# First feed-forward of a macaron decoder block: two output parts by seven block products, weight sums by adding transfers, a smaller ring, and coefficient steps moved into the mix

## Chip, cores and metric

One core of a Trainium2 chip runs the whole decoder block in one program. The metric is the device time of one execution in microseconds, the median of several runs. All inputs are in HBM at the start, the output is in HBM at the end.

## The reference

The layer works on 512 tokens of 1024 channels, all in float32. A vector c gives nine modulation vectors (shift, scale and gate for three sub-layers); then come a SwiGLU feed-forward, a token mixer (pooling and three groups of dilated attention, gated) and a second feed-forward, each added to the residual h.

```python
D_MODEL, SEQ, D_FF = 1024, 512, 2816
cond = jax.nn.silu(c)
mod = cond @ w_ada[l] + b_ada[l]
sh1, sc1, gt1, sh2, sc2, gt2, sh3, sc3, gt3 = [m[:, None, :] for m in jnp.split(mod, 9, axis=-1)]
u = modulate(rmsnorm(h, g_norm_ffn1[l]), sh1, sc1)
h = h + 0.5 * gt1 * swiglu(u, w_ffn1_in[l], w_ffn1_out[l])
u = modulate(rmsnorm(h, g_norm_mix[l]), sh2, sc2)
h = h + gt2 * token_mixing(u, cos, sin, w_in[l], ...)
u = modulate(rmsnorm(h, g_norm_ffn2[l]), sh3, sc3)
h = h + 0.5 * gt3 * swiglu(u, w_ffn2_in[l], w_ffn2_out[l])
...
def swiglu(u, w_in, w_out):
    a, b = jnp.split(u @ w_in, 2, axis=-1)
    return (jax.nn.silu(a) * b) @ w_out
```

## The kernel before

**Precision.** Everything is kept transposed: channels on the 128 partitions, tokens along the free axis. Each float32 product is made of three products of a shorter type: both operands are split into a high and a low part, and TensorE (PE) adds high times high, high times low and low times high in one PSUM bank. `mm3` issues the three for 512 columns (L390 to L392), `product` for 256 (L787 to L789), `out_blocks` for 256 (L929 to L931). A weight chunk is 128x1024, which is eight 128x128 tiles and so 24 matmuls. ACT writes its high part into the ring `whi` (L346) and DVE its low part into `wlo` (L358). Both rings hold 7 x 1024 + 128 columns. `look(n)` splits chunks up to n beyond the next one; `take` hands out the next chunk.

**Loads.** Chunks come from HBM by transfers on the queue of SP (L266) into three buffers `raw` and, in the feed-forwards, two quarters of `X`. Each engine and each queue works strictly in the order in which the program is written out by hand; nothing reorders at run time.

**Feed-forward.** 22 pairs of tiles (a and b of SwiGLU) are made, and after some of them an output part: `PARTS` are tiles 0-4, 4-8, 8-12, 12-16 and 16-22, each multiplied into all eight output tiles and added to h with the gate. The first four pairs of the first feed-forward run in `startup`, pairs 4 and 5 are plain, the others are made two at a time by `duo`: a product of two 2x2 block matrices by seven block products instead of eight (weight rows in two halves, tokens in two halves). For this the weights need sums of chunks: in the first feed-forward DVE makes four per group of four chunks (L283), in the second it makes two, and two more are made by adding transfers issued by POOL (L291). The output parts 0 to 3 of the second feed-forward are made by seven block products too (`out_blocks`); those of the first are plain (L390 to L392 with `HI` and `HK`, H updated by L1053). Before a duo that follows a plain part stands one settling matmul of 240 columns (L396).

**Coefficients.** The modulation vectors are made beside the rest, in 72 steps of DVE (`ada_do`, L417): each reads 128 rows of w_ada (512 KB, `ada_fetch`, L409, on SP), multiplies by cond and sums. `bg` does the next step and fetches ahead into whatever buffers `ada_free` lists; `ada_stop` is where a stage ends. In the first feed-forward all up to 48 are done: from the second output part on, `bg` is called after H updates, with the buffers `cs` and `AR`. The mix does the rest: three in the loop that makes v1 (with `AR`, `uc` and the parts of `v23`), ten beside attention, three more before the gated merge, and eight beside the mix's output (L1703).

**Start of the mix.** `head` makes the first four query and key tiles. `rope_a` copies each to SBUF with a sign (ACT, L1203), swaps 32-row groups by four transfers on SP (L1206), and multiplies the bank by the cosine (DVE, L1208). Then four token blocks of v1 are made (L1462 to L1465); between them DVE finishes the rotation (`rope_b`, L1214 and L1215). Attention scores (L1252) are put into the middle of the next tile's matmuls. The lines of the loop that matter:

```python
for i in ((), (0, 1), (2,), (3,))[n]:
    self.rope_b(*to[i], 1, sw[i])
if n == 1:
    self.ada_free += [self.v23.rearrange("p n f -> p (n f)")[:, i * D:(i + 1) * D] for i in range(2)]
if n:
    self.bg()
```

The angle tables (`trig`) are made by DVE and ACT (sines, L1181 to L1183) in steps of `todo`, which output parts 2 and 3 of the first feed-forward work off.

Of the kernel before, what the change touches and what calls it, by code (L numbers as in the profile page):

```python
# [131 lines left out]
RING = 7 * 1024 + 128  # L132
# [6 lines left out]
BLOCK_PARTS = {0: (), 2: (0, 1, 2, 3)}  # L139
# [19 lines left out]
class Kernel:  # L159
# [6 lines left out]
    def plan(self):  # L166
# [44 lines left out]
        def ffn(n, ins, outs, first):  # L211
# [248 lines left out]
    def sumsq(self, m, src):  # L460
# [5 lines left out]
        s = self.tp.tile([P, T], F32, name="ut")  # L466
# [24 lines left out]

    def norm_t(self, n, k, hs):
        G = self.mod[:, 24 * n + 8 + k:24 * n + 9 + k]
        t = self.tp.tile([P, T], F32, name="ut")
# [52 lines left out]
    def out_tail(self, ms, ksrc, gate, nxt, squares):  # L547
# [3 lines left out]
        tiles, starts, put = {}, {}, []  # L551
# [3 lines left out]
        for h, hs in enumerate((A, Bh)):  # L555
            for m in ms:
# [12 lines left out]
                for i, (hi, lo, uh, ul) in enumerate(ks):  # L569
                    if h == 1 and m == ms[1] and i == 3:  # L570
                        self.stats_t(self.B[6], A)
                    if h == 1 and m == ms[2] and i == 1:
                        self.spread(self.B[6], A)
# [18 lines left out]
    def out_end(self, ms, ksrc, gate):  # L592
# [5 lines left out]
        rA, rB = (b for b in self.B if not any(b is x for x in self.banks))  # L598
# [12 lines left out]
        for h, hs in enumerate((A, Bh)):  # L611
            for m in ms:
# [20 lines left out]
                s = self.tp.tile([P, T], F32, name="ut")[:, :HT]  # L633
# [34 lines left out]
    def head(self, n, banks, table):  # L668
# [9 lines left out]
        for h, hs in enumerate((A, Bh)):  # L678
            for i, (k, which) in enumerate(steps if h == 0 else [(k, both) for k in range(KT)]):
                if h == 0:  # L680
                    stepA(min(i, 5) + 3)
                    if i == 4:
                        self.stats_t(self.B[7], Bh)
                        nc.scalar.preload_act_table(table)
                    if i == 8:
                        self.spread(self.B[7], Bh)
# [13 lines left out]
    def work(self, name, w):  # L700
        return self.wk[name][:, :w] if self.wk else self.fw.tile([P, w], F32, name=name)

    def ffn_post(self, j, s, pb):
        nc = self.nc
        h = self.wk["hf"][:, j % 2 * T:(j % 2 + 1) * T] if self.wk else self.work(("hf", "u3")[j % 2], T)
        nc.vector.tensor_tensor(h, s, pb, op=OP.mult)
        if self.wk:
# [29 lines left out]
    def u_steps(self, n):  # L737
# [21 lines left out]
        if n:  # L759
            adds = [add(a22, a22, a21, OP.subtract), add(a21, a11, a21, OP.subtract), minus(a11, a22, a11),  # L760
                    minus(a12, a12, a11)]
        else:
            adds = [add(a22, a21, a22, OP.add), add(a21, a11, a21, OP.subtract), add(a11, a22, a11, OP.subtract),
                    add(a12, a12, a11, OP.subtract)]
# [26 lines left out]
    def duo(self, n, j, first, last, extra):  # L791
# [4 lines left out]
        sign, add = (-1.0, OP.subtract) if n else (1.0, OP.add)  # L796
# [29 lines left out]
        for i, (bank, u, start) in enumerate(((A, blk(lo4, T1), True), (B, S[0], True), (A, S[1], False),  # L826
                                              (C, blk(hi4, T1), False), (A, S[2], False), (B, S[3], False),
                                              (A, blk(hi4, T2), False))):
            if i == 6:
                v.tensor_tensor(q(c)[:, :, 1, :], r(u3), r(p5), op=add)  # L830

            late = i == 2 and n == 0 and j == PLAIN[0]
            if not late:
                self.look(3 if n and early and i < 4 else 4)
            self.product(bank, u, start, 0 if i else extra)
            self.step()
            if i == 0:
# [6 lines left out]
            elif i == 2:  # L844
                copy(u2, A, sign)
# [4 lines left out]
            elif i == 4:  # L850
                copy(u3, A, sign)
            elif i == 6:
                silu(1, A)
                v.tensor_tensor(q(c)[:, :, 0, :], r(u2), r(B), op=add)
# [29 lines left out]
    def out_blocks(self, k0):  # L884

        nc, v, M = self.nc, self.nc.vector, self.nc.tensor.matmul
        gate = self.mod[:, 64:72]
# [33 lines left out]
        for i, (banks, u, start) in enumerate(((A, 6, True), (B, 5, True), (A, 4, False), (C, 1, False), (A, 3, False),  # L921
# [10 lines left out]
            self.step()  # L932
            for y in range(2):
# [18 lines left out]
    def ffn2(self):  # L952
        self.put, self.now = [], 0
        self.minus = self.mod[:, 0:4]
        self.nc.vector.tensor_scalar(self.minus, self.mod[:, 68:72], -1.0, None, op0=OP.mult)
# [23 lines left out]

    def more(self):  # L980
# [4 lines left out]
    def open_ffn(self, last=False):  # L985
# [5 lines left out]
        self.wk = None  # L991
        if last:
            self.G = [fp.tile([P, 6 * HT], F32R, name=x) for x in ("GI", "GK")]
            self.wide, self.ev = self.fw.tile([P, 9 * HT], F32, name="wide"), self.fw.tile([P, 4 * T], F32, name="ev")
            self.wk = {"sl": self.wide[:, :4 * HT], "hf": self.wide[:, 4 * HT:8 * HT]}
            self.wk.update({x: self.ev[:, i * T:(i + 1) * T] for i, x in enumerate(("p5", "u2", "u3"))})
# [14 lines left out]
    def ffn(self, n, j, last=None):  # L1011
# [10 lines left out]
        for part, (k0, k1) in enumerate(PARTS):  # L1022
# [12 lines left out]
            if part in BLOCK_PARTS[n]:  # L1035
                self.out_blocks(k0)
# [63 lines left out]
    def beside_out(self, part):  # L1100

        if part == 0:
# [10 lines left out]
        if part == len(PARTS) - 1:  # L1113
            assert self.ada_next == 48 and not self.adat, self.ada_next
# [837 lines left out]
```

## Time and profile before

| | us |
|---|---|
| median of three runs | 979.73 |
| lowest, highest | 979.72, 980.12 |
| the profiled execution | 979.58 |
| its span, first to last instruction | 977.7 |
| first feed-forward, with startup | 0 to about 350 |
| mix | about 350 to 640 |
| second feed-forward | about 640 to 977 |

The profiled execution ran at a granted TensorE clock of 0.999. Its span is 1.9 us below its own time. Busy times of PE count overlapping matmuls, so idle time of PE is better read from its waits and from the starts of its instructions than from the share. Times within rows are counted from the start of the span.

### The profile page before, as it was taken

What the parts mean: (1) busy time and instruction counts of PE and PEld (TensorE: products, weight loads), DVE (VectorE), ACT (ScalarE), POOL (GpSimd) and SP (SyncE); (2) the same over time, 40 slices, a digit from 0 to 9 for tenths busy, and PEclk for the clock granted to TensorE, in tenths of its full rate; (3) what the DMA queues carried; (4) which work ended last, traced back from release to release, by engine and by line L of the source; (5) the groups of instructions that cost most, each with busy time, mean ns of one, the idle gap of its engine ahead of it and who ended that gap; (6) DMA issues with size and microseconds to landing.
All of it is one profiled execution on the core that took longest, in us unless ns stands there. A gap on an engine that the chain in (4) does not pass through costs nothing.

```text
span 977.7 us, 17175 instructions
## 1 busy us (share of the span) xinstructions
PE 968.8 (99%) x6973; PEld 896.5 (92%) x6973; DVE 814.8 (83%) x1165; ACT 507.6 (52%) x764; POOL 52.4 (5%) x57
## 2 busy tenths in 40 slices
PE   9999999999999999999999999999999999999997
PEld 7888998989999899778879998998999999999997
DVE  7989979889798776898888876878999888989663
ACT  5453553534445444445645553464766647556553
POOL 0000000000000000005400000000101100110002
PEclk9999999999999999999999999999999999999999
DMA  9857445455563524765243325612857666665612
GB/s 353 280 187 240 152 151 174 170 179 172 175 197 113 147 64 152 245 201 167 72 129 106 104 72 170 222 61 86 207 146 193 167 170 175 161 165 151 162 33 87
DMA packets 48625, 155.43 MB, mean 159 GB/s; under 512 B 6689, under 2 KB 9505, under 8 KB 48546
## 3 DMA queue, kind: packets, MB, share of 16 engines
q1 hardware_dynamic: 44224, 140.18, 44.0%
q0 software_dynamic: 3744, 13.63, 8.1%
q8 instruction: 54, 0.88, 0.4%
q10 hardware_dynamic: 578, 0.53, 0.2%
q14 instruction: 25, 0.20, 0.1%
HBM read 135.29 MB, written 2.24 MB: 141 GB/s over the span
## 4 chain that ended last, share of the span: by engine, by line
PE 94%; DVE 2%; SPq 1%; issue 1%; ACT 1%; POOL 0%; DMA 0%; POOLq 0%; ACTq 0%; DVEq 0%
PE bank L788 13%; PE bank L787 13%; PE bank L789 13%; PE bank L390 12%; PE bank L392 12%; PE bank L391 12%; PE bank L930 3%; PE bank L929 3%; PE bank L931 3%; PE bank L1878 2%; PE bank L1880 1%; PE bank L1882 1%; SPq L1206 1%; PE bank L1550 1%; PE bank L1252 1%; PE bank L1303 1%
## 5 line engine op out<-in xcount | busy, mean ns | idle before, releaser
L358 DVE TENSOR_TENSOR wlo<-raw,whi 128x1024 fp32r<-128x1024 f32 (+4 forms) x156 | 167.7, 1086 | 49.0 <-ACT whi L346 48.8
L787 PE MATMUL bank<-UH,whi 128*128 128x256 f32 x640 | 176.7, 276 | 0.0
L788 PE MATMUL bank<-UL,whi 128*128 128x256 f32 x640 | 176.7, 276 | 0.0
L789 PE MATMUL bank<-UH,wlo 128*128 128x256 f32 x640 | 176.7, 276 | 0.0
L346 ACT ACTIVATE whi<-raw 128x1024 fp32r<-128x1024 f32 (+4 forms) x156 | 144.0, 938 | 41.3 <-DVE raw L283 33.7
L358 DVE TENSOR_TENSOR wlo<-X,whi 128x1024 fp32r<-128x1024 f32 (+3 forms) x124 | 129.2, 1053 | 19.4 <-ACT whi L346 18.9
L346 ACT ACTIVATE whi<-X 128x1024 fp32r<-128x1024 f32 (+3 forms) x124 | 111.4, 921 | 26.5 <-DVE X L283 24.8
L787 PEld LDWEIGHTS bank<-UH,whi 128*128 128x128 f32 x640 | 120.1, 188 | 0.3
L788 PEld LDWEIGHTS bank<-UL,whi 128*128 128x128 f32 x640 | 120.1, 188 | 0.0
L789 PEld LDWEIGHTS bank<-UH,wlo 128*128 128x128 f32 x640 | 120.1, 188 | 0.0
L787 PE MATMUL bank<-SH,whi 128*128 128x256 f32 x408 | 112.6, 276 | 0.0
L788 PE MATMUL bank<-SL,whi 128*128 128x256 f32 x408 | 112.6, 276 | 0.0
L789 PE MATMUL bank<-SH,wlo 128*128 128x256 f32 x408 | 112.6, 276 | 0.0
L390 PE MATMUL bank<-UH,whi 128*128 128x512 f32 (+1 forms) x304 | 105.7, 348 | 0.0
L391 PE MATMUL bank<-UL,whi 128*128 128x512 f32 (+1 forms) x304 | 104.3, 343 | 0.1
L392 PE MATMUL bank<-UH,wlo 128*128 128x512 f32 (+1 forms) x304 | 104.0, 342 | 0.0
L390 PE MATMUL bank<-HI,whi 128*128 128x512 f32 (+1 forms) x278 | 96.4, 347 | 0.0
L391 PE MATMUL bank<-HK,whi 128*128 128x512 f32 (+1 forms) x278 | 96.1, 346 | 0.0
L392 PE MATMUL bank<-HI,wlo 128*128 128x512 f32 (+1 forms) x278 | 96.0, 345 | 0.0
L787 PEld LDWEIGHTS bank<-SH,whi 128*128 128x128 f32 x408 | 76.6, 188 | 0.0
L789 PEld LDWEIGHTS bank<-SH,wlo 128*128 128x128 f32 x408 | 76.6, 188 | 0.0
L788 PEld LDWEIGHTS bank<-SL,whi 128*128 128x128 f32 x408 | 76.6, 188 | 0.0
(385 smaller groups left out, 2140.5 us busy)
## 6 DMA issues: line engine op xcount, KB each, us to landing
raw<-wmix SPq DMA_DIRECT2D x44, 512.0 KB, 3.8
raw<-wf1i SPq DMA_DIRECT2D x31, 512.0 KB, 5.0
raw<-wf2i SPq DMA_DIRECT2D x30, 512.0 KB, 4.3
ada<-wada SPq DMA_DIRECT2D x23, 512.0 KB, 5.7
AR<-wada SPq DMA_DIRECT2D x19, 512.0 KB, 4.2
X<-wf2i SPq DMA_DIRECT2D x14, 512.0 KB, 4.5
X<-raw POOLq DMA_DIRECT2D x13, 512.0 KB, 5.3
cs<-wada SPq DMA_DIRECT2D x12, 512.0 KB, 3.7
```

The lines of the kernel that those rows point to most:

```text
L346: self.nc.scalar.activation(self.hi[:, y], r[:, x], AF.Copy)
L358: self.nc.vector.tensor_tensor(self.lo[:, y], r[:, x], self.hi[:, y], op=OP.subtract)
L390: M(ps, hi, uh, start=start, stop=False)
L391: M(ps, hi, ul, start=False, stop=False)
L392: M(ps, lo, uh, start=False, stop=stop)
L787: M(o, hi, uh, start=start and p == 0 and k == 0, stop=False, skip_group_check=True)
L788: M(o, hi, ul, start=False, stop=False, skip_group_check=True)
L789: M(o, lo, uh, start=False, stop=k == 3, skip_group_check=True)
L929: M(o, hi, uh, start=start and m % 2 == 0 and k == 0, stop=False, skip_group_check=True)
L930: M(o, hi, ul, start=False, stop=False, skip_group_check=True)
L931: M(o, lo, uh, start=False, stop=k == 1, skip_group_check=True)
L1878: M(b, hi, self.UH[k], start=k == 0, stop=False)
```

## The change

- `BLOCK_PARTS` lists parts 2 and 3 for the first feed-forward: their outputs go through `out_blocks`, and the duos before them (8, 10, 12 and 14) also make the sums of hidden blocks that it needs (`block_hidden`). `out_blocks` takes the gate of the feed-forward it serves, and works off one step of `todo` after each product.
- All groups of the first feed-forward have two sums by DVE and two by adding transfers, as the second has. With the two new groups there are ten, so 20 more transfers on POOL. The signs that went with the other form of the sums go.
- The ring has 6 x 1024 + 512 + 128 columns.
- Coefficient steps: the first feed-forward stops at 40 instead of 48. Eight are made in duos 6 and 8 (after products 1, 3, 5 and 6), eight in part 1; in parts 2 and 3 there are none. In the v1 loop of the mix there are two after each of four token blocks, eight instead of three; beside the mix's output there are eleven instead of eight. The angle tables start with part 1.
- Both feed-forwards have the same work tiles; `ev` stands all the time, and the temporary tiles `ut` are thirds of it. Banks that are not in rotation are found by `spare`.

```diff
-RING = 7 * 1024 + 128
+RING = 6 * 1024 + 512 + 128
...
-BLOCK_PARTS = {0: (), 2: (0, 1, 2, 3)}
+BLOCK_PARTS = {0: (2, 3), 2: (0, 1, 2, 3)}
...
-                        blocks(ins[at:at + 4], n == 2)
+                        blocks(ins[at:at + 4], True)
...
+    def ut(self):
+        self.turn = (self.turn + 1) % 3
+        return self.ev[:, self.turn * T:(self.turn + 1) * T]
+
+    def spare(self):
+        return [b for b in self.B if not any(b is x for x in self.banks)]
...
             if not late:
-                self.look(3 if n and early and i < 4 else 4)
+                self.look(3 if early and i < 4 else 4)
             self.product(bank, u, start, 0 if i else extra)
             self.step()
+            if n == 0 and j < PLAIN[0] + 4 and i in (1, 3, 5, 6):
+                self.bg()
...
-    def out_blocks(self, k0):
+    def out_blocks(self, n, k0):
...
-        gate = self.mod[:, 64:72]
+        gate = self.mod[:, 24 * n + 16:24 * n + 24]
...
             self.step()
+            if self.todo:
+                self.todo.pop(0)()
...
-            self.ada_free, self.ada_stop = [self.cs, self.AR], 48
+            self.ada_free, self.ada_stop = [self.cs, self.AR], 40
             self.bg_fetch()
+            self.negate(0)
...
-        if part == 2:
+        if part == 1:
             self.todo = self.trig()
...
-            self.ada_free, self.ada_stop, self.ada_depth = [self.AR, uf], 61, 2
+            self.ada_free, self.ada_stop, self.ada_depth = [self.AR, uf], 58, 2
...
-                if n:
-                    self.bg()
+                self.bg()
+                self.bg()
...
-            self.ada_free, self.ada_stop, self.ada_depth = [self.AR], 64, 1
+            self.ada_free, self.ada_stop, self.ada_depth = [self.AR], 61, 1
...
             kl = [ks(0)]
             do(2)
+            self.bg()
             kl.append(ks(1))
             do()
+            self.bg()
...
-                for _ in range((2, 2, 2, 2, 0)[m]):
+                for _ in range((2, 2, 2, 2, 1)[m]):
                     self.bg()
```

More of the change, by code (lines that the diff above doesn't have):

```diff
@@ L550, in out_tail @@
         nc = self.nc
-        tiles, starts, put = {}, {}, []
+        tiles, starts, put, rest = {}, {}, [], self.spare()
         A, Bh = slice(0, HT), slice(HT, T)
@@ L597, in out_end @@
         A, Bh = slice(0, HT), slice(HT, T)
-        rA, rB = (b for b in self.B if not any(b is x for x in self.banks))
+        rA, rB = self.spare()
         self.held = self.pos
@@ L990, in open_ffn @@
         self.HH, self.HL = ([x[:, i * T:(i + 1) * T] for i in range(NH)] for x in (self.HHall, self.HLall))
[L991 to L996, printed above, removed]
+        self.n, self.G = 2 * last, [fp.tile([P, 6 * HT], F32R, name=x) for x in ("GI", "GK")]
+        self.wide = self.fw.tile([P, 9 * HT], F32, name="wide")
+        self.wk = {"sl": self.wide[:, :4 * HT], "hf": self.wide[:, 4 * HT:8 * HT]}
+        self.wk.update({x: self.ev[:, i * T:(i + 1) * T] for i, x in enumerate(("p5", "u2", "u3"))})
         self.Xall = xp.tile([P, 4 * D], F32, name="X")
@@ L1113, in beside_out @@
         if part == len(PARTS) - 1:
-            assert self.ada_next == 48 and not self.adat, self.ada_next
+            assert self.ada_next == 40 and not self.adat, self.ada_next
             self.ada_free = None
@@ L1515, in mix @@
             self.pool_diff(0, b)
[L1516 to L1517 removed]
+            assert self.ada_next == 58 and not self.adat, self.ada_next
+            self.ada_free, self.ada_stop, self.ada_depth = [self.AR], 61, 1
             self.bg_fetch()
```

50 lines of the change are left out of this document (23 added, 27 removed).

## The prediction

> **What bounds the kernel now.** I read the page's head and its chain first, then who makes TensorE wait, then single stages.
>
> ```profile
> span 977.7 us, 17175 instructions
> PE 968.8 (99%) x6973; PEld 896.5 (92%) x6973; DVE 814.8 (83%) x1165; ACT 507.6 (52%) x764; POOL 52.4 (5%) x57
> PE 94%; DVE 2%; SPq 1%; issue 1%; ACT 1%; POOL 0%; DMA 0%; POOLq 0%; ACTq 0%; DVEq 0%
> ```
>
> Matmul spans overlap, so "busy 99%" alone proves little, but the chain says the same: 94% of the span is matmul following matmul. The waits of PE between 15 and 960 us are two lines in all:
>
> ```profile
> PE bank L1878 <- ACT UH L507: 0.5, 1, 0.5
> PE bank L488 <- DVE r L483: 0.4, 1, 0.4
> ```
>
> So every matmul slot removed is time gained, as long as DVE, ACT and the transfers stay ahead, and every new wait of PE is time lost in full. DVE, at 83%, is the engine that can produce such waits.
>
> **The matmuls that go.** A plain output part of the first feed-forward (96 matmuls of 512 columns: 4 chunks, 8 weight tiles, 3 products) can be compared with a block part of the second (7 products, 8 weight tiles, 3 products: 168 of 256 columns). Start time, duration, instruction:
>
> ```profile
> 200.53 0.40 PE L390 MATMUL bank<-HI,whi 128*128 128x512 f32 x1
> 222.32 0.27 PE L396 MATMUL bank<-UH,whi 128*128 128x240 f32 x1
> 222.43 0.28 PE L787 MATMUL bank<-UH,whi 128*128 128x256 f32 x1
> ...
> 705.56 0.28 PE L929 MATMUL bank<-GI,whi 128*128 128x256 f32 x1
> 724.60 0.28 PE L787 MATMUL bank<-UH,whi 128*128 128x256 f32 x1
> ```
>
> The plain part lasts 222.32 - 200.53 = 21.79 us (227 ns a matmul), the block part 724.60 - 705.56 = 19.04 us (113 ns). Two parts change: 2 x 2.75 = 5.50 us. The settling matmul after each (222.43 - 222.32 = 0.11) goes as well: 0.22. Gain 5.72 us, all of it on the path.
>
> The Trainium skill ("TensorE: Matmul & The Clock Gate", Back-to-back issue gap) has a rule against this: in streams of weight load and matmul it gives some 81 ns for 128 columns and 131 for 512, so halving the columns would not halve the slot. A straight line between its two figures gives an estimate of 98 ns for 256 columns, 168 x 98 = 16.5 us against 96 x 131 = 12.6, a loss of 7.8 us in two parts. The rows above speak against it.
>
> **DVE in the first feed-forward.** Busy time by stage (columns: PE, PEld, DVE, ACT, POOL): duo 6, duo 8, the output of part 1, that of part 2, then a block part and two duos of the second feed-forward.
>
> ```profile
> 102.40:121.50 19.10, 19.10 (x170) 19.10 (x169) 19.07 (x20) 11.45 (x15) 0.00 (x0) 1.00 0.49 157
> 121.50:140.50 19.00, 19.00 (x170) 19.00 (x169) 14.93 (x17) 11.28 (x15) 0.00 (x0) 1.00 0.51 156
> 140.50:162.40 21.90, 21.90 (x99) 18.14 (x99) 18.60 (x25) 5.66 (x7) 0.00 (x0) 1.00 0.51 161
> 200.50:222.40 21.90, 21.90 (x99) 18.14 (x98) 19.17 (x29) 5.57 (x6) 0.00 (x0) 1.00 0.56 176
> 705.50:724.60 19.10, 19.10 (x170) 19.10 (x170) 18.72 (x25) 14.42 (x20) 1.88 (x3) 1.00 0.73 195
> 724.60:762.70 38.10, 38.10 (x339) 38.10 (x338) 35.31 (x44) 20.80 (x28) 4.17 (x5) 1.00 0.68 170
> ...
> 163.91 1.22 DVE L358 TENSOR_TENSOR wlo<-raw,whi 128x1024 fp32r<-128x1024 f32 x1
> ```
>
> Ops of 128x1024 follow each other every 1.14 us (in the mix rows below, 386.75 - 385.61). Duos 6 and 8 lose two sums a group (4 x 1.14) and get eight coefficient steps (8 x 1.14): 34.0 - 4.6 + 9.1 = 38.5 of 38.1 us. Part 1 now has the angle-table steps (19.17, as in part 2 before) and the block sums of duo 8, taken as at most 2.5 such ops, 2.9: 22.1 of 21.9. That is 0.6 us too much. The cover is the lead of the weight splits: the one at 163.91 ends at 165.13, and PE takes it as the fourth chunk of a duo that began at 162.44, at 162.44 + 3 x 2.72 = 170.6, 5.5 us later. Duos 10 and 12 have 35.31 + 2 x 1.14 = 37.6 of 38.1 and do not lose more. Cost 0. Without the cover: the 0.6 and one product, 2.72, so 3.3 us.
>
> The 20 adding transfers run on POOL, which has nothing else there (0.00 in four rows). The second feed-forward already makes its sums this way with five buffers and PE did not wait, so 0. The sines move in front of two bank copies of part 2:
>
> ```profile
> 269.57 0.31 ACT L1181 ACTIVATE tr<-tr 128x128 f32<-128x128 f32 x1 [6.27 <-DVE tr L1177]
> 270.23 0.29 ACT L1183 ACTIVATE tr<-tr 128x128 f32<-128x128 f32 x1
> ```
>
> They take 1.0 us; ACT has 4.7 us free in a block part (14.42 of 19.10). Taken as 0, at most 1.0. The ring of 6.6 chunks still holds the six that a look-ahead of 4 needs: 0. Names in place of pools: 0.
>
> **The coefficient steps that move to the mix.** Eight of them leave the first feed-forward. Three go to the mix's output, where DVE idles before an H update: cost 0, and if that idle time were gone 3.4 us.
>
> ```profile
> 606.44 0.75 DVE L1703 SCALAR_TENSOR_TENSOR H<-bank,mod,H 128x512 f32<-128x512 f32 x1 [4.60 <-PE bank L392]
> ```
>
> Five go into the loop that makes v1, between head and attention. There the rotary swaps occupy SP and DVE feeds the first scores (L1252):
>
> ```profile
> 378.54 1.28 DVE L1208 TENSOR_TENSOR k<-bank,cs 128x512 f32<-128x512 f32 x2
> 381.81 1.22 DVE L358 TENSOR_TENSOR wlo<-raw,whi 128x1024 fp32r<-128x1024 f32 x1 [2.00 <-ACT whi L346]
> 385.61 1.22 DVE L417 SCALAR_TENSOR_TENSOR AR<-AR,cond 128x1024 f32<-128x1024 f32 x1
> 386.75 1.22 DVE L358 TENSOR_TENSOR wlo<-raw,whi 128x1024 fp32r<-128x1024 f32 x1
> 387.89 0.69 DVE L1214 TENSOR_TENSOR k<-k,cs 128x512 f32<-128x512 f32 x1
> 389.22 1.22 DVE L417 SCALAR_TENSOR_TENSOR uc<-uc,cond 128x1024 f32<-128x1024 f32 x1
> 390.36 1.29 DVE L358 TENSOR_TENSOR wlo<-raw,whi 128x256 fp32r<-128x256 f32 x2
> 391.57 0.69 DVE L1214 TENSOR_TENSOR k<-k,cs 128x512 f32<-128x512 f32 x1
> 392.90 1.22 DVE L417 SCALAR_TENSOR_TENSOR v<-v,cond 128x1024 f32<-128x1024 f32 x1
> ```
>
> ```profile
> 377.33 4.99 SPq L1206 DMA_DIRECT2D q<-v  x8
> 382.41 4.96 SPq L1206 DMA_DIRECT2D k<-v  x8
> 387.48 0.53 SPq L266 DMA_DIRECT2D raw<-wmix  x1
> 388.05 0.46 SPq L409 DMA_DIRECT2D v<-wada  x1
> 388.60 0.38 SPq L266 DMA_DIRECT2D raw<-wmix  x1
> 389.16 0.33 SPq L409 DMA_DIRECT2D v<-wada  x1
> ```
>
> ```profile
> 392.29 0.70 DVE k L1215
> 393.04 0.49 PE bank L1252 x4
> ...
> 391.33 1.06 ACT L346 ACTIVATE whi<-raw 128x1024 fp32r<-128x1024 f32 x1 [1.86 <-DMA raw<-wmix]
> ...
> DMA to landing us min/median/max: 4.6/6.4/7.2
> ```
>
> (The last line is that of the coefficient loads from 385 to 402 us.) The chain already ran from the last key rotation to the scores: PE starts them at 393.04. In the changed order, as built, DVE does AR and uc after the four L1208, the chunk split, the two q rotations, then **AR and uc again**, a split, the first k rotation, v and v, a split, the last k rotation. The second AR load stands on SP behind all 16 swaps, so its earliest slot is 387.48. What waits on DVE behind it: both k rotations, and for these PE. Working in the old trace's times (the part before is shorter by 5.72 for all engines alike):
>
> - First pair: 2.3 us from 379.8, into an idle time of 2.00. DVE is ready for the second AR at about 385.8.
> - AR lands when the load of that slot landed: 391.3 (the ACT row). DVE stands 5.5 us. AR done 392.4.
> - uc lands 388.05 + 4.6 = 392.65, done 393.8; split 394.9; first k rotation (389.22 - 387.89 = 1.33) 396.3.
> - v, fourth load: 389.16 + 7.2 = 396.35, done 397.5. The other v, fifth load: one more step of (396.35 - 392.65)/2, 398.2, done 399.35.
> - Split in two pieces (391.57 - 390.36 = 1.21) 400.55; last k rotation 401.9.
>
> That end stood at 392.90. PE's scores start 9.0 us later, and PE, in order, has nothing it may do meanwhile. Bounds: if no load after AR is waited for, the work behind it is 5 x 1.14 + 1.21 + 2 x 1.33 = 9.6, end 400.9, 8.0 us. If the fifth load takes 7.2 and two steps more, 11. [...] No row excludes a follow-on: the two steps after the last rotation delay the masks. I take 0 and keep 1.5 as an end.
>
> **The sum.** -5.72 + 9.0 = +3.3 us. The profiled execution took 979.58 (span 977.7 and 1.9 around it), so 982.9; the median of the runs is 979.73, 0.15 above. Forecast 983.0, a little slower.
>
> **Rivals.**
> - *The loads come in time* (faster). If the second AR and uc were there at 385.8, the loop would cost its added work alone: four steps before the last rotation, 4.6 less the 2.0 of idle time, 2.6 us, and the sum is 979.73 - 5.72 + 2.6 = 976.6; with no stall at all 974.0. For it: PE's waits in the old mix are tiny. Against it: the swaps hold SP from 377.33 to 387.4 without a gap. It decides when the stall is under 3.8 us (-5.72 + 3.8 is the edge of 0.2%). Chance 0.12.
> - *A half-size stall*, 3.8 to 7.7 us, about 979.7, if loads land faster or DVE has less to do: 0.07.
> - *DVE overruns in the first feed-forward too*: 0.6 us over its capacity before part 2, coefficient loads in two buffers between weight loads on one queue, adding transfers before a split can begin. If the lead of 5.5 us is used up, PE loses up to 3.3 us: 979.73 - 5.72 + 9.0 + 3.3 = 986.3, and 987.8 with the follow-on: 0.15.
> - *Shorter matmuls save nothing*: if each were held to its weight load, near the same slot for 256 and 512 columns, the parts would be longer. The equal rows 19.04 and 21.79 exclude it nearly: 0.01. The issue-gap section of the Trainium skill's TensorE page named above would have it so.
> - The forecast: 0.65.
>
> **How the numbers follow.** 0.2% is 2.0 us, about what a measurement of this kernel can tell from no change. Slower: 0.65 + 0.15 + 0.01 = 0.81; same 0.07; faster 0.12. The range leaves out the faster rival and most of the half-size one: low 981.0 (a stall of 7.0). High 987.0 (a stall of 11 with the follow-on gives 986.5, the third rival 986.3 to 987.8).
>
> **What would show it.** Right: first-feed-forward output parts 2 and 3 at 19.0 us each with no PE gap; in the v1 loop DVE waiting about 5 us for AR from its load (a new line among the waits), and PE idle before L1252 by 8 to 11 us. Wrong: scores that start within 4 us of the end of the matmuls before them; AR issued before the k swaps; PE gaps between 102 and 320 us; or parts 2 and 3 not shorter than 21 us.

## The result and the profile after

The changed kernel takes 986.06 us (median of four runs, 985.71 to 987.01); the kernel before takes 979.92 (979.72 to 980.13) beside it. The ratio is 1.0064, 95% interval 1.0047 to 1.0082: slower by 6.1 us, where 983.0 was forecast. In several of the experiments below some executions of one kernel take 5 to 11 us longer than its others; their number is given, because it is part of what had to be explained.

The head of the page of the changed kernel, with its chain:

```profile
span 983.7 us, 17626 instructions
PE 966.1 (98%) x7115; PEld 900.2 (92%) x7115; DVE 824.7 (84%) x1190; ACT 525.2 (53%) x784; POOL 69.7 (7%) x77
PE 81%; DVE 9%; DMA 4%; issue 3%; ACT 2%; SPq 1%; POOL 0%; POOLq 0%; ACTq 0%; DVEq 0%
```

PE fell from 94% of the chain to 81%; DVE, transfers and "issue" took its place. The waits of PE between 15 and 960 us (total, times, longest) say where:

```profile
PE bank L1259 <- issue: 4.1, 1, 4.1
PE bank L1259 <- DVE k L1222: 4.0, 1, 4.0
PE bank L1888 <- ACT UH L514: 0.5, 1, 0.5
PE bank L789 <- ACT bank L796: 0.5, 1, 0.5
PE bank L488 <- DVE r L483: 0.5, 1, 0.5
```

L1259 are the scores (L1252 before). The lines L1888 and L488 are those that stood there before (then L1878 and L488); two waits at the scores and one at a duo product (L789) are new. Windows of the same execution (columns: length, PE, PEld, DVE, ACT, POOL, granted clock, transfer share, GB/s): duo 6, duo 8, output part 1, parts 2 and 3, then the stretch around the scores.

```profile
102.60:121.66 19.06, 19.06 (x170) 19.06 (x169) 17.30 (x20) 11.45 (x16) 1.73 (x2) 1.00 0.84 255
121.66:141.40 19.74, 19.29 (x170) 19.09 (x169) 19.04 (x26) 11.31 (x15) 0.89 (x1) 1.00 0.86 275
141.46:163.25 21.79, 21.79 (x99) 18.02 (x97) 20.95 (x34) 7.37 (x8) 1.70 (x2) 1.00 0.75 252
201.45:220.49 19.04, 19.04 (x171) 19.04 (x169) 17.99 (x25) 15.30 (x24) 1.29 (x3) 1.00 0.70 173
258.57:277.61 19.04, 19.04 (x171) 19.04 (x169) 16.05 (x19) 13.59 (x19) 1.72 (x2) 1.00 0.68 168
387.30:391.70 4.40, 0.35 (x2) 0.02 (x1) 4.33 (x8) 1.06 (x1) 0.00 (x0) 0.92 0.98 360
391.70:392.10 0.40, 0.39 (x4) 0.40 (x4) 0.40 (x1) 0.00 (x0) 0.00 (x0) 0.50 0.67 164
392.10:396.50 4.40, 0.43 (x6) 0.13 (x4) 4.37 (x9) 0.00 (x0) 0.00 (x0) 0.50 0.92 327
396.50:401.30 4.80, 4.80 (x14) 3.71 (x15) 3.94 (x9) 0.00 (x0) 0.00 (x0) 0.50 0.79 270
```

Parts 2 and 3 take 19.04 us each without a gap. PE is idle twice for 4.4 us at the scores, DVE being busy all that time, and then runs at a granted clock of 0.50: 14 matmuls in 4.80 us. PE starts none of the matmuls behind the scores in these waits. The section on the kernel before says that nothing reorders at run time. For these matmuls that holds, for weight loads it is too strong: one weight load of the second scores starts at 396.66 us, ahead of the matmul of the load before it at 396.86.

The difference of 6.0 us between the spans (983.7 - 977.7) can be followed by how much later each stage starts than in the trace of before:

| | us |
|---|---|
| start of the first feed-forward's own products (58.99, before 58.83) | +0.16 |
| duos 6 and 8 (38.84, before 38.09) | +0.75 |
| output parts 2 and 3 with their settling matmuls | -5.72 |
| wait of the first scores | +8.58 |
| the 24 matmuls behind it, at half clock in part (7.48, before 5.58) | +1.90 |
| first duo of the second feed-forward (19.45, before 19.05) | +0.40 |
| sum | +6.07 |

The first row is not an effect of the change that the runs could tell from chance: that start lies between 58.8 and 60.0 us in the thirteen profiles.

At the scores DVE and SP of the changed kernel read (start, duration, instruction, and in brackets the idle time before it and what ended it):

```profile
372.50 5.00 SPq L1213 DMA_DIRECT2D q<-v  x8
377.59 4.97 SPq L1213 DMA_DIRECT2D k<-v  x8
382.66 0.53 SPq L409 DMA_DIRECT2D AR<-wada  x1
```

```profile
386.65 1.22 DVE L417 SCALAR_TENSOR_TENSOR AR<-AR,cond 128x1024 f32<-128x1024 f32 x1 [5.58 <-DMA AR<-wada]
...
387.92 1.23 DVE L417 SCALAR_TENSOR_TENSOR uc<-uc,cond 128x1024 f32<-128x1024 f32 x1
...
391.53 1.22 DVE L417 SCALAR_TENSOR_TENSOR v<-v,cond 128x1024 f32<-128x1024 f32 x1
...
395.75 0.69 DVE L1222 TENSOR_TENSOR k<-k,k 128x512 f32<-128x512 f32 x1
...
398.40 1.22 DVE L417 SCALAR_TENSOR_TENSOR uc<-uc,cond 128x1024 f32<-128x1024 f32 x1 [0.82 <-DMA uc<-wada]
```

The load of AR is issued the moment the sixteen swaps are through, and DVE stands 5.58 us for it. The last key rotation (L1222) ends at 396.4, and with it the second wait of the scores; the wait for uc at 398.40 comes after that and holds up no score.

### The profile page after: what moved, and what is told of

Read it like the earlier page. It is cut to its first block, busy times and chain, and to the rows that moved or that the text cites. A ratio compares the mean times of both kernels' runs of the same rounds, so it can differ in the third digit from the quotient of the medians.

```text
span 983.7 us, 17626 instructions
## 1 busy us (share of the span) xinstructions
PE 966.1 (98%) x7115; PEld 900.2 (92%) x7115; DVE 824.7 (84%) x1190; ACT 525.2 (53%) x784; POOL 69.7 (7%) x77
## 4 chain that ended last, share of the span: by engine, by line
PE 81%; DVE 9%; DMA 4%; issue 3%; ACT 2%; SPq 1%; POOL 0%; POOLq 0%; ACTq 0%; DVEq 0%
PE bank L789 12%; PE bank L790 12%; PE bank L791 12%; PE bank L390 9%; PE bank L391 9%; PE bank L392 9%; PE bank L933 4%; PE bank L934 4%; PE bank L932 4%; DVE ada L417 3%; DVE wlo L358 2%; DVE UL L528 1%; SPq L1213 1%; PE bank L1259 1%; ACT whi L346 1%
## 5 line engine op out<-in xcount | busy, mean ns | idle before, releaser
L358 DVE TENSOR_TENSOR wlo<-raw,whi 128x1024 fp32r<-128x1024 f32 (+3 forms) x156 | 169.2, 1095 | 46.2 <-ACT whi L346 45.9
L789 PE MATMUL bank<-UH,whi 128*128 128x256 f32 x640 | 176.8, 276 | 0.1
L346 ACT ACTIVATE whi<-raw 128x1024 fp32r<-128x1024 f32 (+3 forms) x156 | 143.8, 938 | 23.1 <-DVE raw L283 10.5
L358 DVE TENSOR_TENSOR wlo<-X,whi 128x1024 fp32r<-128x1024 f32 (+3 forms) x123 | 135.6, 1112 | 21.9 <-ACT whi L346 20.6
L346 ACT ACTIVATE whi<-X 128x1024 fp32r<-128x1024 f32 (+3 forms) x123 | 117.2, 970 | 24.8 <-DVE X L283 17.4
L789 PEld LDWEIGHTS bank<-UH,whi 128*128 128x128 f32 x640 | 120.1, 188 | 0.5 <-ACT ev L796 0.3
L789 PE MATMUL bank<-SH,whi 128*128 128x256 f32 x408 | 112.7, 276 | 0.5 <-ACT bank L796 0.5
L789 PEld LDWEIGHTS bank<-SH,whi 128*128 128x128 f32 x408 | 76.6, 188 | 0.7 <-ACT bank L796 0.7
L390 PE MATMUL bank<-HI,whi 128*128 128x512 f32 (+1 forms) x214 | 71.5, 334 | 0.0
L391 PE MATMUL bank<-HK,whi 128*128 128x512 f32 (+1 forms) x214 | 71.1, 332 | 0.0
L392 PE MATMUL bank<-HI,wlo 128*128 128x512 f32 (+1 forms) x214 | 71.1, 332 | 0.0
```

The lines of the kernel that those rows point to most:

```text
L346: self.nc.scalar.activation(self.hi[:, y], r[:, x], AF.Copy)
L358: self.nc.vector.tensor_tensor(self.lo[:, y], r[:, x], self.hi[:, y], op=OP.subtract)
L390: M(ps, hi, uh, start=start, stop=False)
L391: M(ps, hi, ul, start=False, stop=False)
L392: M(ps, lo, uh, start=False, stop=stop)
L789: M(o, hi, uh, start=start and p == 0 and k == 0, stop=False, skip_group_check=True)
```

## The experiments

All runs have a run of the kernel before beside them (980.03 us in the first four, 980.72 in the next four, 980.06 and 980.33 in the last three). E1 to E11 are eleven kernels; diffs are against the changed kernel unless said otherwise.

### E1: the eight steps in late duos

Theory: the loss sits at the v1 loop alone, because DVE and the loads are late there. Rivals: DVE is full wherever the steps go, or the stall has another cause.

```diff
-            self.ada_free, self.ada_stop = [self.cs, self.AR], 40
+            self.ada_free, self.ada_stop = [self.cs, self.AR], 48
...
-            if n == 0 and j < PLAIN[0] + 4 and i in (1, 3, 5, 6):
+            if n == 0 and ((j < PLAIN[0] + 4 or j >= 18) and i in (1, 3, 5, 6)):
                 self.bg()
```

(The loop, the stops of the mix and its output are as before the change again.)

> The eight coefficient steps that the change put into the v1 loop (five) and in front of the mix output (three) go into the duos 18 and 20 of the first feed-forward, four each; the rest is the changed kernel. Theory: the changed kernel loses at the v1 loop alone, 8.6 us of waiting and about 1.9 us at half clock behind it, and the block products keep their 5.7 us: 986.06 - 8.6 - 1.9 = 975.6 us, the scores of L1259 wait under 1 us in all and the granted clock stays at 1.00 there. Rival 1, VectorE is full in the duos already: each of the duos 18 and 20 pays what duo 8 paid (0.75 us), 977.1 us. Rival 2, the stall at the v1 loop comes from something else than the five steps (the tables of the rotation, the smaller ring): the wait stays and the time stays above 984.

Measured: 975.90 us median of ten. Eight executions lie at 975.0 to 976.7, two at 984.9 and 986.1; the ratio over all ten is 0.9976 (0.9949 to 1.0002). The profiled execution took 975.35 us, with a span of 973.6. Its waits of PE:

```profile
PE bank L1886 <- ACT UH L514: 0.5, 1, 0.5
PE bank L488 <- DVE r L483: 0.5, 1, 0.5
PE bank L789 <- ACT ev L796: 0.4, 1, 0.4
```

The scores no longer wait, the clock stays at 1.00, and duos 18 and 20 keep their pace: the theory's number, 975.6, and neither rival's. That it comes so close is in part a balance: in this profile duos 6 and 8 lose nothing (38.09 us), but the start is 0.92 us later than in the changed kernel's profile. What is left is a wait at L789 of 0.4 us in the first duo of the second feed-forward, which takes 19.72 us here (19.45 in the changed kernel, 19.05 before the change), and the two long executions.

### E2: the steps spread over all duos

```diff
-            if n == 0 and ((j < PLAIN[0] + 4 or j >= 18) and i in (1, 3, 5, 6)):
+            if n == 0 and (i in (1, 5)):
```

(against E1)

> As the run before, but all sixteen steps of the duos spread evenly, two in each of the eight duos 6 to 20. Theory: duo 8 of the changed kernel lost 0.75 us because its four steps and their reloads stood ahead of weight loads and splits; with two a duo the slack of the others covers it and all eight duos take 38.1 us: 975.6 - 0.75 = 974.8 us. Rival: it is any coefficient load in SP's queue ahead of a weight load that costs, or the adding transfers alone; then several duos lose 0.4 to 0.75 us each and the time is 976 to 979.

Measured: 978.76 us (976.98 to 987.74; ratio 0.9998, 0.9978 to 1.0018). Duo 8 has no gap, but PE waits in two later stages, the block output of part 2 (212.4 us) and duo 16 (251.5 us).

```profile
PE bank L789 <- ACT ev L796: 1.3, 1, 1.3
PE bank L932 <- ACT ev L891: 0.7, 1, 0.7
```

In front of both waits ACT, in order, had stood for the sums of hidden blocks that DVE makes (L880), with the bank copies behind it (and, at the first wait, one of the angle-table steps, 1.0 us, between them):

```profile
209.08 1.06 ACT L881 ACTIVATE HI<-wide 128x1024 fp32r<-128x1024 f32 x1 [2.91 <-DVE wide L880]
...
249.33 1.06 ACT L881 ACTIVATE HI<-wide 128x1024 fp32r<-128x1024 f32 x1 [2.67 <-DVE wide L880]
```

So the rival's number holds, by another mechanism than the one I gave it: not the loads, but DVE, which is late with those sums when it has steps beside them. Duos 18 and 20 have no such sums, and E1 pays nothing there.

### E3: five loads ahead of the swaps

```diff
-            self.ada_free, self.ada_stop, self.ada_depth = [self.AR, uf], 58, 2
+            self.ada_free, self.ada_stop, self.ada_depth = [self.AR, uf, *x], 48, 5
...
+            self.ada_free = [self.AR] + [self.v23.rearrange("p n f -> p (n f)")[:, i * D:(i + 1) * D] for i in range(2)]
+            self.ada_stop, self.ada_depth = 58, 2
+            self.bg_fetch()
```

> The changed kernel with all eight steps in the v1 loop, but five of their loads ahead of the sixteen rotation swaps in SP's queue (into three tiles that are free there), instead of two. VectorE does the same work. Theory, the load behind the swaps is what is late: VectorE no longer waits 5.58, 0.82 and 0.56 us for loads, the scores wait 8.6 - 7.0 = 1.6 us (up to 3 with the swaps 1 us later), the clock does not fall: 986.06 - 7.0 - 1.9 = 977.2 us (977 to 979). Rival, the five added steps fill VectorE itself: the scores still wait 7 us or more, and the time is 984 or more.

Measured: 982.58 us (981.93 to 989.93; ratio 1.0032, 1.0019 to 1.0046). Neither number. In the v1 loop of the profile the long wait for AR is gone, DVE works from 379.5 to 392.0 almost without a pause, and yet PE stands 4.1 us, 3.8 more than before the change:

```profile
387.95:392.05 4.10, 0.29 (x4) 0.10 (x3) 4.01 (x9) 0.74 (x1) 0.00 (x0) 1.00 1.02 404
392.05:395.75 3.70, 3.70 (x12) 2.81 (x13) 3.27 (x6) 0.32 (x1) 0.00 (x0) 0.54 0.99 345
750.00:800.00 50.00, 50.00 (x427) 50.00 (x426) 45.96 (x57) 30.38 (x41) 4.33 (x5) 1.00 0.63 163
800.00:850.00 50.00, 50.00 (x427) 50.00 (x426) 42.31 (x53) 30.34 (x41) 4.36 (x5) 1.00 0.62 154
```

So of the stall of 8.58 us the late load makes 4.8 and the added steps 3.8, in the order in which E3 issues its loads and with the 1 us or so that its swaps are later. My 1.6 subtracted three waits from the stall, of which two (0.82 and 0.56) lie behind the last rotation and never held up a score; that leaves 3.0, and the swaps, now behind five loads, landed about 1 us later (DVE waits 0.96 us for q). One idle time of 4.1 us is enough for the fall of the clock (0.54). The two last lines belong to another matter: this profile is of one of the long executions (989.93). The changed kernel does 443 and 444 matmuls in the same two windows, this one 427, at a granted clock of 1.00. From start to start that is 117.8 ns a matmul instead of 113.3.

### E4: matmuls in the wait

```diff
+        if not kind and not n:
+            for _ in range(18):
+                nc.tensor.matmul(self.bO, self.UH[0][:, :P], self.UH[0], start=True, stop=True, skip_group_check=True)
```

(in front of the scores)

> The changed kernel with 18 extra matmuls of 512 columns (18 x 0.227 = 4.1 us) on TensorE in front of each of the two scores that wait 4.4 us; nothing reads what they make. They lie within the waits, so the stall itself stays at 8.6 us. Theory, the half clock behind the stall is set off by TensorE standing idle: the ten matmuls of 427 ns take 227 again, 986.06 - 1.9 = 984.1 us. Rival, the clock falls there for another reason (total work, another engine): granted clock 0.5 stays and the time is 986.1 or more.

Measured: 985.29 us (983.93 to 985.78; ratio 1.0052, 1.0037 to 1.0067). The stretch from the scores on:

```profile
388.75:394.45 5.70, 4.24 (x19) 3.22 (x18) 5.00 (x8) 1.06 (x1) 0.00 (x0) 1.00 0.79 271
394.45:399.65 5.20, 5.20 (x26) 3.90 (x26) 5.17 (x9) 0.00 (x0) 0.00 (x0) 1.00 0.87 311
399.65:405.25 5.60, 5.60 (x27) 4.58 (x26) 5.42 (x18) 1.79 (x9) 0.00 (x0) 1.00 0.91 352
```

The clock never falls, and the tile behind the scores takes 5.59 us instead of 7.48. The half clock is thus set off by PE standing idle. The total did not fall by the full 1.9 us since in this execution the load of AR came 1.5 us later (DVE waited 7.07) and duo 8 lost 1.69 us; the first duo of the second feed-forward lost nothing (19.05).

### E5, E6: against the long executions

In the profile of E3 the matmuls of 117.8 ns begin just behind an idle time of 0.6 us in the first duo of the second feed-forward and last until the block products end: 2,038 x 4.5 ns = 9.2 us. E5 puts a settling matmul there; E6 also moves steps out of duos 6 and 8.

```diff
+            if p and again is not None:
+                self.settle(again, w[4][0], self.UH[0])
```

(in `product`, for the seventh product of that duo, against E1)

```diff
-            if n == 0 and ((j < PLAIN[0] + 4 or j >= 18) and i in (1, 3, 5, 6)):
+            if n == 0 and (i in ((3, 6) if j < PLAIN[0] + 4 else (1, 3, 5, 6) if j >= 16 else ())):
```

(E6, against E5)

> The first run (steps in duos 18 and 20) with one more settling matmul of 240 columns in the second feed-forward: in its first duo, halfway through the seventh product, just behind the place where TensorE stood 0.27 to 0.7 us for a bank copy. Two of ten executions of the first run took 985 to 986 us, the others 975.0 to 976.7. In the one long execution that a profile shows (early loads), every 256-column matmul from that place to the end of the block products runs at 117.8 ns instead of 113.3: 2,038 x 4.5 ns = 9.2 us. Theory: an idle of TensorE there lets the matmuls go on at the longer pace, and a settling matmul brings the shorter one back: all executions at 975.9 + 0.1 = 976 us, none above 978. Rival 1, the pace is decided elsewhere: again some two in ten at 985. Rival 2, the extra matmul itself sets the wrong pace: most at 985.

> As the run before, with the coefficient steps thinned in the duos 6 and 8 (two each instead of four) and four each in duos 16, 18 and 20, which make no operands for the block output. Theory: duo 8 lost 0.6 to 1.7 us in three of the profiles because its four steps and their reloads hold up weight loads; with two steps it keeps 38.1 us and the time is 975.2 to 976. Rival: the adding transfers alone make that gap, or duo 16 now pays: 976 to 977.5.

Measured: E5 984.70 us (975.91 to 986.93; ratio 1.0024, 1.0001 to 1.0048), E6 984.41 (975.73 to 986.07; ratio 1.0014, 0.9990 to 1.0039). Of twelve executions each, eight lie at 984.2 to 986.9 and four at 975.7 to 977.8. The settling matmul made the long pace more frequent: rival 2. The profile of E6 is of a long one. PE is idle for 0.3 us at 698.1, the matmuls of 117.8 ns begin right behind the settling matmul at 700.0, and they end with the block products. The profile of E5 is of a short one: there the longer pace begins behind the idle time, at 700.1, and ends at 702.3, soon after the settling matmul at 701.6, as the theory had it. In E6 duo 8 had no gap in the profile, but duos 18 and 20 took 38.5 us instead of 38.1; in E5 duo 8 lost 1.8 us; the short executions are no faster than E1's, so whether thinner steps help there is not settled.

### E7, E8: the ring, and the block outputs, each by itself

```diff
-RING = 7 * 1024 + 128
+RING = 6 * 1024 + 512 + 128
```

(E7, against the kernel before)

```diff
-BLOCK_PARTS = {0: (2, 3), 2: (0, 1, 2, 3)}
+BLOCK_PARTS = {0: (), 2: (0, 1, 2, 3)}
```

(E8)

> The kernel before, with nothing changed but the ring of split weights (6 x 1024 + 640 instead of 7 x 1024 + 128 columns). Theory: the ring costs nothing anywhere, 980.0 us, and the 0.4 us that the changed kernel lost in the first duo of the second feed-forward comes from when the first adding transfer lands (8.2 us after its issue instead of 7.4). Rival: with the smaller ring the splits have less lead there, TensorE waits 0.3 to 0.7 us for the bank copy in this kernel too, and some executions fall into the longer pace: 980.4, with some at 989.

> The changed kernel with its output parts 2 and 3 of the first feed-forward as plain products again (21.79 us each); its duos still make block products without added operands of the output. The theory, 5.7 us gained by the seven block products: 986.06 + 5.7 = 991.8 us. Rival, the operands that the duos must make for them, and the longer queue on VectorE, cost part of it back: then the duos 10 to 14 or duo 8 get shorter here and the time is 989 to 991. As parts 2 and 3 then have room for coefficient steps between their products, the steps of the duos 6 and 8 stay where they are and those of part 1 too.

Measured: E7 980.13 us (979.52 to 981.0; ratio 0.9993, 0.9984 to 1.0002), no wait in the second feed-forward: the ring costs nothing. E8 992.13 us (990.95 to 993.36; ratio 1.0116, 1.0103 to 1.0129), 6.1 us above the changed kernel, or 5.3 if each is counted from the kernel before beside it, where 5.7 was expected; its plain part 2 takes 21.79 us, as before. In its profile the first duo of the second feed-forward has no gap either.

### E9: bank copies ahead of splits

What makes PE wait in that duo? In the changed kernel (ACT, then POOL, then the split of the kernel before):

```profile
698.54 1.06 ACT L346 ACTIVATE whi<-raw 128x1024 fp32r<-128x1024 f32 x1 [1.83 <-DMA raw<-raw]
707.08 1.15 ACT L346 ACTIVATE whi<-X 128x512 fp32r<-128x512 f32 x2
708.13 0.59 ACT L796 ACTIVATE ev<-bank 128x512 f32<-128x512 f32 x1
...
690.32 0.92 POOL L291 DMA_DIRECT2D raw<-raw  x1 [207.86 <-DVE X L283]
...
692.14 1.07 ACT L346 ACTIVATE whi<-raw 128x1024 fp32r<-128x1024 f32 x1 [1.09 <-DMA raw<-raw]
```

A split waits for the first adding transfer. Counted from the first matmul of the second feed-forward (653.85, before 648.20), the split starts at 44.69 us instead of 43.94 and the bank copy at 54.28 instead of 53.54: everything on ACT is 0.7 us later, and PE's seventh product needs that bank. Duo 8 of the first feed-forward shows the same order:

```profile
126.14 1.06 ACT L346 ACTIVATE whi<-X 128x1024 fp32r<-128x1024 f32 x1 [3.66 <-DMA X<-raw]
127.11 0.58 ACT L796 ACTIVATE bank<-bank 128x512 f32<-128x512 f32 x1
```

```profile
127.01 0.28 PE L791 MATMUL bank<-SH,wlo 128*128 128x256 f32 x1
127.74 0.38 PE L789 MATMUL bank<-SH,whi 128*128 128x256 f32 x1 [0.45 <-ACT bank L796]
```

```diff
-            late = i == 2 and n == 0 and j == PLAIN[0]
+            late = (n, j, i) in ((0, PLAIN[0], 2), (0, PLAIN[0] + 2, 0), (2, PLAIN[2], 4))
...
+            if late:
+                self.look(3 if i == 2 else 4)
```

(behind the copies, against E1)

> The first run (steps in duos 18 and 20, without the extra settling matmul) with two splits put behind a bank copy in ScalarE's order instead of ahead of it: in duo 8 after the first product, and in the first duo of the second feed-forward after the fifth. Theory: TensorE stands there only because the in-order ScalarE holds the copy behind a split that waits for an adding transfer; without that hold both duos take their full pace (38.09 and 19.05 us) whenever the transfer lands, and as TensorE does not idle in the second feed-forward, no execution falls to the 117.8 ns pace: 975.9 - 0.5 = 975.2 to 975.6 us, none above 978. Rival: the splits then come too late for their own products, the wait moves two products on, and some executions still take 985.

Measured: 976.11 us (974.65 to 986.12; ratio 0.9978, 0.9956 to 1.0000), three of twelve executions at 983 to 986. Duo 8 has no gap in the profile (38.12 for both duos). But E1, E2, E6 and E11 have none either, without the swap, so E9 alone proves nothing for duo 8; the landings in the eleven profiles decide it (in the section on why the prediction was right or wrong). In the second feed-forward the rival's number holds, though not its place: the transfer landed later still (ACT waited 2.89 us for it instead of 1.83), and PE now waits for a copy two products earlier (0.4 us), not later, and in the block output behind (0.4 us).

### E10, E11: the fetch of instructions

The first adding transfer is issued 36.4 to 36.8 us after the second feed-forward's first matmul in every profile, and the split that waits for it starts at 43.7 to 43.9 us in some kernels and at 44.7 to 45.0 in others (45.8 in E9). What differs is when one packet of 16 KB in the queue q8, "instruction", starts: at 42.2 to 42.6 us where the transfer is late, but at 42.8 to 43.3 in the kernel before, E7 and E8, where it is in time. A shift of a few tenths of a microsecond would thus decide. In windows of 2 us (queue, packets, MB, share of 16 engines), the changed kernel from 42.0 us after the start of that stage, and E10 from 30.0:

```profile
q0 software_dynamic: 108, 0.38, 98.4%
q8 instruction: 1, 0.02, 2.9%
```

```profile
q1 hardware_dynamic: 117, 0.41, 51.5%
q8 instruction: 1, 0.02, 3.1%
q14 instruction: 1, 0.01, 1.0%
```

2.9% of 16 engines over 2 us is 0.94 us on one of them, among the packets of the adding transfer (q0). E4, whose 36 added matmuls moved that packet to 31.3 us, had no gap. The Trainium skill ("Runtime: NRT & Kernel Launch", Instruction fetch mechanics) says that an engine's instructions come in blocks of 16 KiB, 256 instructions, by a DMA queue of the engine's own; the packets of q8 agree (16,384 bytes each, one every 14.4 us on average in the block products of the changed kernel, where 128 matmuls and as many weight loads take 14.5).

E10 has 36 matmuls of 128 columns in front of the first scores, as E4 had of 512, but in E1. E11 has twelve passes only, where PE waits anyway:

```diff
-                if k == 3:
-                    warm(1, self.H[k])
+                if k < KT - 1:
+                    warm((3, 2)[k > 3], self.H[k])
...
-        warm(5, self.H[7])
+        warm(7, self.H[7])
```

(E11, in the start, against E1)

> The first run with 36 extra matmuls of 128 columns in front of the first scores; nothing reads what they make. They cost 36 x 0.06 to 0.11 = 2 to 4 us there. They also move the fetches of TensorE's instructions (one packet of 16 KB for 256 instructions) ahead: in the profiles the fetch near the first adding transfer of the second feed-forward starts 42.4 to 42.6 us after that stage's start where the transfer lands late (44.7 to 45.0, six kernels), and at 42.8, 43.25, 43.29 or 31.3 us where it lands at 43.7 to 43.9 (four kernels). Theory: that packet, 0.9 us long on one DMA engine, is what makes the transfer late. Here it starts near 31 us, the transfer lands at 43.8 us, TensorE does not wait in that duo (19.05 us), and no execution takes 9 us more than the others: 977.5 to 980 us, all within 2 us. Rival: the landing follows from something else (addresses, the load beside it): it stays at 44.7 to 45.0 and one execution in five takes 9 us more.

> The first run (steps in duos 18 and 20) with six more of the kernel's warming matmuls in the start, in places where TensorE waits 0.48 to 0.60 us anyway: two behind the fourth input tile, two behind the sixth, two before the first product (each is two passes of 128 columns, twelve passes in all); nothing reads what they make. The 36 passes of the run before moved the fetch of TensorE's instructions from 42.6 to 31.1 us after the start of the second feed-forward, 0.32 us for one; twelve should bring it to 38.8 us, and it takes 0.95 us, while the packets of the first adding transfer begin at 40.2. Theory: the transfer lands at 43.8 us, that duo takes 19.05 us and no execution takes 9 us more; the other stages are those of the first run: 975.9 - 0.6 = 975.3 us (974.5 to 977, all within 3 us). Rival 1: the fetch is moved too little and the landing stays at 44.7 to 45.0, with one execution in five at 985. Rival 2: the fetches of the first feed-forward, moved too, now hit a transfer there: 0.5 to 2 us more in a duo.

Measured: E10 979.24 us (978.58 to 981.29, eleven executions, ten of them within 1.1 us; ratio 0.9991, 0.9982 to 1.0000). The added matmuls cost 3.9 us, and duos 6 and 8 lost 1.4. Its packet starts at 31.1 us, and the split that waits reads:

```profile
692.02 1.07 ACT L346 ACTIVATE whi<-raw 128x1024 fp32r<-128x1024 f32 x1 [0.92 <-DMA raw<-raw]
```

That is 43.8 us after the stage's start; the duo takes 19.05 us. E11: **975.35 us** (974.72 to 975.57, five executions; ratio 0.9948, 0.9935 to 0.9962), faster than both kernels. Its packet starts at 37.9 us, well ahead of the transfer's packets (40.3), and yet the split starts at 44.3, half a microsecond later than in E10, so the packet is not all that moves the landing. The duo takes 19.07 us. Of all waits of PE between 15 and 960 us one is left:

```profile
PE bank L488 <- DVE r L483: 0.4, 1, 0.4
```

E11 is not shown to be faster than E1's short executions (975.0 to 976.7): in the two profiles it gains 0.7 us in that duo and loses 0.6 at the start of the mix, where its matmuls run at 117.8 ns.

E1, E2, E3, E5, E6 and E9, whose profiles show PE idle in that duo, had 24 long executions of 64; E4, E7, E8, E10 and E11, whose profiles show none there, had none of 34, and the kernel before had none of 88. The changed kernel has the gap and had none in four. There is one profile for each kernel, so this is a link and no proof; the five executions of E11 alone, against two long ones of ten in E1, would not show it.

## Why the prediction was right or wrong

**The block outputs: right.** 19.04 us each, 5.72 with the settling matmuls. E8 gives 5.3 to 6.1 back. The rival of the issue gap falls: 168 matmuls of 256 columns in 19.04 us are 113 ns each, in the first feed-forward as in the second.

**DVE in the first feed-forward: cost 0 was wrong, by another path.** The load on DVE was less than I had added up (17.30 + 19.04 = 36.3 us in duos 6 and 8 instead of 38.5; 20.95 in part 1 instead of 22.1), and in the changed kernel the lead of the splits held (in E2, where DVE gets steps beside the hidden sums, it is late with those sums). The 0.75 us came from "20 adding transfers on POOL: 0": POOL had room, but a split waits for each of them on ACT, and a bank copy stands behind the split. E9, which swaps the two, has no gap in duo 8 in its profile; E1 and E6 have none there without the swap, so the gap comes and goes with when the transfer lands. The profiles bear this out. Counted from the settling matmul in front of duo 6, the split that waits starts at 22.1 to 23.0 us in E1, E2, E3, E6 and E11, and PE stands under 0.1 us; it starts at 23.5, 23.6, 24.1, 24.3 and 24.7 in E8, the changed kernel, E4, E10 and E5, and PE stands 0.5, 0.6, 1.0, 0.9 and 1.7 us. Why the transfer lands later in some kernels stays open.

**Second feed-forward: "PE did not wait, so 0" was wrong by 0.4.** It makes its sums exactly as before; the packet of instructions that started at 43.25 us of this stage now starts at 42.48, and the first adding transfer lands 0.7 us later. E10 moves the packet out of the way and the wait goes; but its 36 matmuls change other times too, and E11's landing at 44.3 us shows that the packet is not the whole of it.

**The ring, the three steps at the mix's output: 0, right.** E7 shows the one; at the other the output takes 32.66 us in the changed kernel and 32.67 before.

**The wait for AR: right.** Forecast 5.5 us, measured 5.58. Behind it uc and the first two v loads were in time, where I had put about 1.0 us of small waits (401.9 against 400.9), and the work behind it took 9.8 us instead of 9.6: the stall is 8.58 instead of 9.0.

**What the stall is made of.** The edge that the prediction drew, loads in time or not, is real but not sharp: with the load in time the added work alone costs 3.8 us in E3, against 2.6 in the rival, the difference being, by the rows, about the 1 us by which E3's swaps are later. E3 still paid 1.4 us for the clock in the tile behind the scores; whether a stall of 2.6 us would have, no run shows.

**The follow-on, taken as 0: wrong, 1.90 us.** The prediction had the masks behind the rotation in mind. It was PE's clock: two idle times of 4.4 us, then 0.50. The Trainium skill ("TensorE: Matmul & The Clock Gate", Part 1) has this as its rule for idle times of over some 3.4 us, at half rate until as much time has been busy; 4.1 and 4.4 us here agree, and E4 shows the cause. The end of 1.5 that I kept for an unknown follow-on was nearly its size.

Together: the forecast's +3.3 lacks 0.16 + 0.75 + 1.90 + 0.40 and has 0.42 too much at the stall, so +6.1 in the spans. The order of the causes was right; three small terms of one sign were put at 0.

**Where it was luck.** The time is 3.1 us above the forecast and 0.9 under the upper end of the range. That end came from a stall of 11 us with a follow-on of 1.5, and the stall was 8.58; that the terms put at 0 fitted into the room is in part luck. The third rival, DVE overrunning in the first feed-forward too, gives 986.3, nearly the measured number, but by another sum: it puts 3.3 us there, where 0.75 was lost, and nothing on the clock. And one of the prediction's own signs of being wrong came true, a PE gap between 102 and 320 us: the one in duo 8.

## What to carry to other kernels

A step that is free by an engine's busy share is not free at its place: see which load it needs, what that load queues behind, and which engine holds its results back in order; here the five steps added to the v1 loop cost 10.5 us (8.58 + 1.90), and all eight moved steps cost nothing in two late duos. If TensorE will stand for 4 us, add the cost of its clock (1.4 and 1.9 us here). A transfer that another engine waits for in order needs a margin of a microsecond, since packets that the program does not name, such as instructions, can fall into it.

## What the runs showed of the hardware

- TensorE's granted clock fell to 0.50 after idle times of 4.1 to 4.4 us and came back after 3.7 to 4.8 us of work; ten 512-column matmuls took 427 ns instead of 227.
- The same stream of weight loads and 256-column matmuls has two paces at a granted clock of 1.00: 113.3 and 117.8 ns. In E3 the longer one follows an idle time of 0.6 us, in E6 the settling matmul behind one of 0.3, and it held for over 2,000 matmuls both times, which costs 9 us. All long executions are of kernels whose profiles show PE idle in that duo. But idle time is neither needed nor enough: in E10 the longer pace begins at 119.2 us with no idle time in front of it and ends behind one of 0.9 us at 127.7, and in E1 and the changed kernel the shorter pace goes on behind idle times of 0.5 and 0.3 us in that duo. What decides between the paces, and why the settling matmul made the longer one more frequent, stays open.
- 36 more matmuls at 390 us moved a fetch of TensorE's instructions at 685 us by 11.5 us, and with it an adding transfer of 512 KB landed 1.2 us earlier (43.8 us after the stage's start in E10, 45.0 in E1). The fetch takes 0.94 us on one DMA engine; that it is the whole cause is not shown, since in E11 the transfer landed at 44.3 with the fetch out of its way.
